# FFN up projection by seven quarter products instead of eight, in a two-layer float32 step

## The chip, the cores and the metric

The kernel runs on one core of one Trainium2 chip. The metric is device time in microseconds (us) from one launch to its end; lower is better. The core has five engines that run side by side, each from its own queue, in order: PE multiplies matrices, DVE and ACT and POOL do elementwise work, SP issues transfers (DMA). [...]

## The reference, cut to what matters

The program is a two-layer decoder step over 1024 prompt tokens and 64 sample tokens, 1088 columns in all. Layer 0 mixes by a recurrence (RWKV), layer 1 by latent attention. Each layer then projects with `w_o`, adds to the residual stream, and runs a gated FFN with a short convolution on the gate:

```python
D_MODEL, D_FF, CONV_W = 1024, 2816, 3

def conv_glu(xn, conv_prev, w_up, conv_w, conv_b, w_down):
    u = xn @ w_up                                  # 1024 x 5632
    gate, val = u[..., :D_FF], u[..., D_FF:]
    ext = concatenate([conv_prev, gate], axis=1)
    conv = conv_b
    for j in range(CONV_W):
        conv = conv + ext[:, j:j + T] * conv_w[j]
    h = silu(conv) * val
    return h @ w_down, ext[:, T:]

# in each layer:
x = x + concatenate([o_tok, o_mem], -1) @ w_o[l]
f, c = conv_glu(rms_norm(x, norm_ffn[l]), ...)
x = x + f
```

## The kernel before, in words

The residual stream lies in SBUF as `x`, 128 partitions x 8 feature blocks x 1088 tokens. All large products are made in float32 precision by splitting each operand in a high and a low part (`wh`, `wl` and `xh`, `xl`, type float32r) and adding three products: `wh*xh + wh*xl + wl*xh`. So a 128 x 128 weight block costs three matmuls for each group of tokens, `gemm_y` at L474 to L476. The split of a weight is a cast on ACT (L207) and a subtraction on DVE (L208; in the first stage, the recurrence, it runs on POOL). The helper `split` (L1130, L1131) does the same for activations. Tokens are taken in three groups `G3` of 364, 364 and 360 columns.

One FFN has 22 chunks of 128 hidden features. For a chunk, `up` loads the gate weights and the value weights (`load_w`, 1024 x 128 each, in two pieces of 256 KB), multiplies the gate (eight blocks of 128 features, three token groups), copies it to `ext` (ACT), runs the convolution over all tokens (DVE, L1300 to L1302), takes SiLU (ACT), multiplies the value part, forms the product and splits it to `hh`, `hl`. Chunks go in six groups of 4, 4, 4, 4, 3, 3. While a group is projected up, the group before it is projected down (`gemm_x`), each result added to `x` by DVE (`residual`, L1159). `merge` interleaves the two streams in program order, by steps and weights:

```python
for i in range(len(groups)):
    u = ups(i)
    if i:
        s.merge([(down(i - 1), 24), (s.take(u, 110), 110)])
    s.drain(u)
return (yield from down_last())
```

The first group has no down projection beside it, and the last down projection (`down_last`) has no up projection beside it. Ahead of the FFN stands the `w_o` projection, whose squares are summed on POOL (`acc`, L1168) for the norm; `norm_x` then scales and splits `x` for the FFN. Behind it stands, in layer 0, the split of `x` for the latent projections, and in layer 1 the final norm. The framework orders the instructions of each engine from the program by its own scheduler; the order tables below show what came out. PSUM has four buffers `mm`, two `dn` and two `tp` in this phase.

Of the kernel before, what the change touches and what calls it, by code (L numbers as in the profile page):

```python
# [85 lines left out]
G3 = [(0, 364), (364, 364), (728, 360)]  # L86
NH = 6
# [10 lines left out]
class Step:  # L98
# [1006 lines left out]
    def load_stream(s, xd, i):  # L1105
        c0, n = G3[i]
        s.tc.keep_in_program_order(s.nc.scalar.dma_start(out=s.x[:, :, c0:c0 + n], in_=xd.rearrange("(k p) t -> p k t", p=128)[:, :, c0:c0 + n]))
# [32 lines left out]
    def load_x(s, first):  # L1140

        nc, x = s.nc, s.x
        for i in range(9):
            rows = 128 if i < 8 else 64
            xt = first[i] if i < len(first) else s.x_tile(i, nc.sync)
            for h in range(2):
                q = s.pst("tp")
                for k in range(4):
                    nc.tensor.transpose(q[:, k * 128:k * 128 + rows], xt[:rows, 512 * h + 128 * k:512 * h + 128 * k + 128], s.ident[:rows, :rows])
                qv = q.rearrange("p (k t) -> p k t", t=128)[:, :, :rows]  # L1150
                nc.scalar.copy(x[:, 4 * h:4 * h + 4, 128 * i:128 * i + rows], qv)
            yield

    def residual(s, d, g, p, acc):
# [7 lines left out]
        a = acc[c0][:, :n]  # L1162
        if d == 0:
            nc.scalar.activation(a, xv, AF.Square)
        else:
            sq = s.st([128, 364], "nt", s.ntb)
# [3 lines left out]
    def last_acc(s):  # L1170

        return s.t(s.wp, [128, 4, 128], "wr", 3).rearrange("p a b -> p (a b)")

    def scales(s, g, acc):
# [4 lines left out]
        nc.tensor.matmul(q[:, :n], s.mean1k, acc[c0][:, :n], start=True, stop=True)  # L1179
        r = s.rstd[c0] = s.t(s.xp, [128, 364], "rstd", 3)[:, :n]  # L1180
# [3 lines left out]
    def norm_x(s, g, acc, gain, xs):  # L1184

        nc = s.nc
        c0, n = g
        for _ in range(s.LAG):
            yield
        s.scales(g, acc)  # L1190
        for k in range(KC):
            xh, xl = xs[k]
            t = s.st([128, 364], "nt", s.ntb)
            nc.vector.scalar_tensor_tensor(t[:, :n], s.x[:, k, c0:c0 + n], s.pv(gain[0], gain[1] + k), s.rstd[c0], ALU.mult, ALU.mult)
            s.split(xh[:, :n], xl[:, :n], t[:, :n])
            yield

    def split_x(s, g, acc, xs):

        c0, n = g  # L1200
        for k in range(KC):
# [3 lines left out]
            if k == s.LAG and g != G3[2]:  # L1205
                s.scales(g, acc)
        if g == G3[2]:
# [3 lines left out]
    def new_xg(s):  # L1211

        xh, xl = (s.t(s.xp, [128, KC, 364], n, 3, F32R) for n in ("xh", "xl"))
        return [(xh[:, k], xl[:, k]) for k in range(KC)]

    def gemm_x(s, wf, xs):

        for d in range(KC):
            w = wf(d)
            for g in G3:  # L1220
                p = s.pst("dn")
                s.drain(s.gemm_y(p, w, xs, *g))
                s.residual(d, g, p, None)
                yield

    def gemm_t(s, ws, d0, xs, acc, after=None, ahead=(), m=8):

        def part(g, x, c0):  # L1230
            for j, w in enumerate(ws):
                p = s.pst("mm")
                s.drain(s.gemm_y(p, w, x, c0, g[1]))
                s.residual(d0 + j, g, p, acc)
# [3 lines left out]
        for i, z in enumerate(xs):  # L1238
            yield from s.mergeg([(part(*z), len(ws)), (pend, m)] + [(a, 8) for a in ahead[i:i + 1]])
            if after:  # L1240
                pend = after(z[0], acc)
        return pend

    def ffn(s, l, xs, pend, after, pre=None):
# [3 lines left out]
        W, Wd = I["w_ffn_up"][l], I["w_ffn_down"][l]  # L1248
        NCH = DFF // 128

# [4 lines left out]
        for i in range(0, NCH, 4):  # L1255
            m = min(4, NCH - i)
            stg = s.st([18, 512], "cvst", 2)
# [3 lines left out]
        nc.scalar.copy(cprev.rearrange("p c b -> p (c b)"), q[:, :16 * NCH])  # L1261

        def up(c, out):
            wg = s.load_w([(W[:, 128 * c:128 * c + 128], 0, 128)])
            if c == 0:
                wv = s.load_w([(W[:, DFF:DFF + 128], 0, 128)])
            yield
            ext = s.st([128, 1106], "ext", 1)
            nc.gpsimd.memset(ext[:, 0:2], 0.0)
            es = ext[:, 1026:1106].rearrange("p (b t) -> p b t", t=10)  # L1270
            nc.gpsimd.tensor_copy(es[:, :, 0:2], cprev[:, c].rearrange("p (b j) -> p b j", j=2))

            def gate(i):
                c0, n = G3[i]
                p = s.pst("mm")
                yield from s.gemm_y(p, wg, xs[i], 0, n)
                m = min(n, NP_ - c0)
                nc.scalar.copy(ext[:, 2 + c0:2 + c0 + m], p[:, :m])  # L1278
                if m < n:
                    nc.scalar.copy(es[:, :, 2:10], p[:, m:n].rearrange("p (b t) -> p b t", t=8))  # L1280

            def val(i):
                p = s.pst("mm")
                yield from s.gemm_y(p, wv, xs[i], 0, G3[i][1])
                ps[i] = p

            ps = {}
            if c == 0:
                for _ in s.seq(gate(0), gate(1), val(0), val(1)):
                    next(pend, None)  # L1290
                    yield
                s.drain(pend)
                yield from gate(2)
            else:
                for i in range(3):
                    yield from gate(i)
            cv = s.st([128, 1106], "cv", 1)
            w = [s.pv(f"conv_w{l}{j}", c) for j in range(3)]
            cv = cv[:, :1104]
            nc.vector.tensor_scalar(cv, ext[:, 0:1104], w[0], s.pv(f"conv_b{l}", c), ALU.mult, ALU.add)  # L1300
            nc.vector.scalar_tensor_tensor(cv, ext[:, 1:1105], w[1], cv, ALU.mult, ALU.add)
            nc.vector.scalar_tensor_tensor(cv, ext[:, 2:1106], w[2], cv, ALU.mult, ALU.add)  # L1302
            nc.scalar.activation(cv, cv, AF.Silu)
            nc.gpsimd.tensor_copy(cout[:, c, 0:2], ext[:, 1024:1026])  # L1304
            nc.gpsimd.tensor_copy(cout[:, c, 2:18].rearrange("p (b j) -> p b j", j=2), es[:, :, 8:10])
            if c:
                wv = s.load_w([(W[:, DFF + 128 * c:DFF + 128 * c + 128], 0, 128)])
            yield
            h, lo = s.st([128, NT], "hh", 6, F32R), s.st([128, NT], "hl", 6, F32R)
            out.append((h, lo))  # L1310
            for i, (c0, n) in enumerate(G3):
                if i not in ps:
                    yield from val(i)
                p = ps.pop(i)
                m = min(n, NP_ - c0)
                t = s.st([128, 364], "nt", s.ntb)
                nc.vector.tensor_tensor(t[:, :m], cv[:, c0:c0 + m], p[:, :m], ALU.mult)
                if m < n:
                    sv = s.bc(cv[:, 1026:1027], [10, 8], [1, 8])
                    nc.vector.tensor_tensor(t[:, m:n].rearrange("p (b t) -> p b t", t=8), sv, p[:, m:n].rearrange("p (b t) -> p b t", t=8), ALU.mult)  # L1320
                s.split(h[:, c0:c0 + n], lo[:, c0:c0 + n], t[:, :n])
                yield

        groups = [(0, 4), (4, 4), (8, 4), (12, 4), (16, 3), (19, 3)]
        hs = {}

        def ups(i):
            c0, n = groups[i]
            hs[i] = []
            for c in range(c0, c0 + n):  # L1330
                yield from up(c, hs[i])

        def down(i):
# [970 lines left out]
```

## Time and profile before

| what | value |
|---|---|
| time, median of 3 runs | 3498.66 us (3494.58 to 3508.95) |
| time of the profiled execution | 3513.38 us |
| its span in the trace | 3511.6 us |
| PE busy in the span | 3368.6 us |
| DVE, ACT, POOL busy | 1790.5, 1298.7, 457.7 us |

The span is what the trace covers from the first to the last instruction. PE's matmuls overlap in the trace (a matmul of 364 columns is shown with some 0.33 us while the next one starts 0.166 us later), so PE's cost is read from the distance between starts, or from a count of matmuls in a stretch in which PE never stops. The layer-0 `w_o` and FFN stage runs from about 985 to 1915 us, that of layer 1 from about 2590 us to the end.

### The profile page before, as it was taken

The page shows a single profiled execution, that of the slowest core. Times are in us where ns is not written, and L with a number is a line of the kernel's source. Part 1 is how long each engine was busy: PE and PEld are TensorE (multiplying, and loading weights), DVE is VectorE, ACT ScalarE, POOL GpSimd, SP SyncE. Part 2 cuts the span into 40 slices and gives each one's busy share as a digit, 9 for nine tenths or more (in the row PEclk, how much of TensorE's full clock was granted, in tenths as well). Part 3 has the DMA queues.
Part 4 walks back from the last instruction along what each step waited for, and adds up shares of the span by engine and source line. Part 5 has one row for each costly group of instructions (what it writes and reads, how often), then busy time and mean ns, then how long its engine had stood idle before and what let it go on. Part 6 is the DMA issues. An engine that isn't in the chain of part 4 may idle for free. (4 is left out here: it accounts for less than half of the span.)

```text
span 3511.6 us, 58202 instructions
## 1 busy us (share of the span) xinstructions
PE 3368.6 (96%) x23112; PEld 2899.4 (83%) x23112; DVE 1790.5 (51%) x4242; ACT 1298.7 (37%) x2971; POOL 457.7 (13%) x767
## 2 busy tenths in 40 slices
PE   6999999999889999999999999899999999999998
PEld 5555677775579999999999888655579999999998
DVE  5776676775535343333345477434445433343344
ACT  5555445543544222212225455333334312222222
POOL 4323133331011000000003001011111000000000
PEclk9998699998889999999999999899999999999999
DMA  4212011113141111111113102345321111111112
GB/s 119 56 39 76 22 39 41 38 47 95 51 153 48 43 49 43 43 46 46 44 46 111 53 28 70 123 163 179 121 75 42 49 49 40 46 46 43 47 44 78
DMA packets 299284, 227.13 MB, mean 65 GB/s; under 512 B 40890, under 2 KB 278222, under 8 KB 294916
## 3 DMA queue, kind: packets, MB, share of 16 engines
q1 hardware_dynamic: 285220, 166.82, 16.3%
q0 software_dynamic: 9888, 51.93, 4.2%
q10 hardware_dynamic: 3904, 4.65, 0.4%
q8 instruction: 182, 2.98, 0.3%
q14 instruction: 90, 0.74, 0.1%
HBM read 197.59 MB, written 25.76 MB: 64 GB/s over the span
## 5 line engine op out<-in xcount | busy, mean ns | idle before, releaser
L474 PE MATMUL pmm<-xh,wh 128*128 128x364 f32 (+2 forms) x2664 | 882.3, 331 | 7.5 <-ACT wh L207 4.8
L476 PE MATMUL pmm<-xh,wl 128*128 128x364 f32 (+2 forms) x2664 | 875.1, 328 | 0.0
L475 PE MATMUL pmm<-xl,wh 128*128 128x364 f32 (+2 forms) x2664 | 872.9, 328 | 0.3
L474 PEld LDWEIGHTS pmm<-xh,wh 128*128 128x128 f32 (+1 forms) x2664 | 500.1, 188 | 12.4 <-ACT wh L207 5.1
L475 PEld LDWEIGHTS pmm<-xl,wh 128*128 128x128 f32 (+1 forms) x2664 | 500.6, 188 | 3.0 <-DVE xl L1434 0.8
L476 PEld LDWEIGHTS pmm<-xh,wl 128*128 128x128 f32 (+1 forms) x2664 | 500.8, 188 | 1.4 <-DVE wl L208 0.2
L207 ACT CAST wh<-wr 128x512 fp32r<-128x512 f32 (+3 forms) x399 | 238.5, 603 | 561.1 <-PE pmm L475 333.4
L208 DVE TENSOR_TENSOR wl<-wr,wh 128x512 fp32r<-128x512 f32 (+2 forms) x307 | 205.0, 670 | 369.9 <-ACT wh L207 369.3
L1159 DVE TENSOR_TENSOR x<-x,pdn 128x364 f32<-128x364 f32 (+1 forms) x240 | 127.4, 531 | 419.2 <-PE pdn L476 419.2
L476 PE MATMUL pdn<-hh,wl 128*128 128x364 f32 (+1 forms) x912 | 300.2, 329 | 0.0
L475 PE MATMUL pdn<-hl,wh 128*128 128x364 f32 (+1 forms) x912 | 298.7, 328 | 0.0
L474 PE MATMUL pdn<-hh,wh 128*128 128x364 f32 (+1 forms) x912 | 298.3, 327 | 0.0
L474 PE MATMUL pmm<-xn,wh 128*128 128x292 f32 (+2 forms) x552 | 207.0, 375 | 3.7 <-DVE e L504 3.7
L475 PE MATMUL pmm<-xn,wh 128*128 128x292 f32 (+2 forms) x552 | 196.9, 357 | 0.0
L476 PE MATMUL pmm<-xn,wl 128*128 128x292 f32 (+2 forms) x552 | 195.5, 355 | 0.6 <-POOL wl L208 0.6
L1278 ACT COPY ext<-pmm 128x364 f32<-128x364 f32 x132 | 58.7, 444 | 364.0 <-PE pmm L476 364.0
L1304 POOL COPY cout<-ext 128x2 f32<-128x2 f32 x44 | 16.9, 385 | 1261.2 <-ACT ext L1278 1261.2
L476 PEld LDWEIGHTS pdn<-hh,wl 128*128 128x128 f32 x912 | 171.3, 188 | 1.1
L475 PEld LDWEIGHTS pdn<-hl,wh 128*128 128x128 f32 x912 | 171.3, 188 | 0.0
L474 PEld LDWEIGHTS pdn<-hh,wh 128*128 128x128 f32 x912 | 171.2, 188 | 0.0
L208 POOL TENSOR_TENSOR wl<-wr,wh 128x512 fp32r<-128x512 f32 (+1 forms) x92 | 121.7, 1325 | 195.9 <-ACT wh L207 163.8
L474 PEld LDWEIGHTS pmm<-xn,wh 128*128 128x128 f32 (+1 forms) x552 | 106.5, 193 | 27.9 <-issue 11.0
(720 smaller groups left out, 5984.1 us busy)
## 6 DMA issues: line engine op xcount, KB each, us to landing
wr<-in_w_ffn_up SPq DMA_DIRECT2D x176, 256.0 KB
wr<-in_w_in_a SPq DMA_DIRECT2D x84, 256.0 KB
wr<-in_w_ffn_down SPq DMA_DIRECT2D x64, 256.0 KB
wr<-in_w_o SPq DMA_DIRECT2D x32, 256.0 KB
wr<-in_w_ffn_down SPq DMA_DIRECT2D x32, 192.0 KB
xl<-odp POOLq DMA_DIRECT2D x4, 1456.0 KB
e<-in_x_prompt SPq DMA_DIRECT2D x16, 256.0 KB
out_y_p<-xl SPq DMA_DIRECT2D x8, 512.0 KB
```

The source lines that it names most:

```text
L207: nc.scalar.copy(wh[:, :n, :m], wr[:, :n, :m])
L208: s.wl_eng.tensor_tensor(wl[:, :n, :m], wr[:, :n, :m], wh[:, :n, :m].bitcast(F32), ALU.subtract)
L474: nc.tensor.matmul(ps[:m, :n], wh[:, :m], xh[:, c0:c0 + n], start=(k == 0), stop=False)
L475: nc.tensor.matmul(ps[:m, :n], wh[:, :m], xl[:, c0:c0 + n], start=False, stop=False)
L476: nc.tensor.matmul(ps[:m, :n], wl[:, :m], xh[:, c0:c0 + n], start=False, stop=(k == last))
L1159: nc.vector.tensor_tensor(xv, xv, p[:, :n], ALU.add)
L1278: nc.scalar.copy(ext[:, 2 + c0:2 + c0 + m], p[:, :m])
L1304: nc.gpsimd.tensor_copy(cout[:, c, 0:2], ext[:, 1024:1026])
```

## The change

The up projection of a chunk is now made for half of the tokens at a time (544), and the half is cut in two quarters of 272 tokens. Gate and value blocks, two halves of the 1024 input features and two token quarters make a 2 x 2 by 2 x 2 block product. It is formed by seven products of combined blocks (Winograd's form of Strassen's scheme) where eight were used. With weights `v1, g1` (first 512 features) and `v2, g2` (last 512) and quarters `lo`, `hi`:

- `load_up` makes four combined weights on POOL (L1281: `s1 = g1 + g2`, `s2 = s1 - v1`, `v1 - g1`, `v2 - s2`) and splits seven weights (ACT L1276, DVE L1277).
- `combine_x` makes the seven combined operands of a half once: DVE scales `x` (L1204), POOL forms four differences (L1207 to L1210), ACT and DVE split all seven. The two halves use the same seven buffers.
- `up` makes seven products of 4 feature blocks x 3 matmuls x 272 columns each (L1333 to L1335) and adds them up on DVE from PSUM and on POOL (L1340). Convolution, SiLU and the product with the value follow on 544 columns (560 in the second half, with the sample tokens).

The 22 chunks are walked twice, once for each half, so all up and down weights are loaded and split twice. The down projection, `w_o` and the latent projections work on quarters of 272 columns as well. In `w_o`, half 0 is projected first, then half 1 while `combine_x` prepares half 0 for the FFN. `combine_x` for half 1 is the beginning of that half's first group of chunks, beside the last down projection of half 0. PSUM is laid out as six `mm` and two `dn`. The core of the diff:

```diff
+    def combine_x(s, h, gain, xs):
+        nc = s.nc
+        xs += [s.new_xq() for _ in range(7)]
+        lo, hi = slice(0, QT), slice(QT, HT)
+        for j in range(4):
+            a = []
+            for k in (j, j + 4):
+                a.append(s.st([128, HT], "tw", 2))
+                nc.vector.scalar_tensor_tensor(a[-1], s.x[:, k, HT * h:HT * h + HT], s.pv(gain[0], gain[1] + k), s.rstd[h], ALU.mult, ALU.mult)
+            yield
+            t = [s.st([128, QT], "nt", s.ntb) for _ in range(4)]
+            nc.gpsimd.tensor_tensor(t[0], a[0][:, hi], a[0][:, lo], ALU.subtract)
+            nc.gpsimd.tensor_tensor(t[1], a[1][:, hi], t[0], ALU.subtract)
+            nc.gpsimd.tensor_tensor(t[2], a[1][:, hi], a[0][:, hi], ALU.subtract)
+            nc.gpsimd.tensor_tensor(t[3], a[1][:, lo], t[1], ALU.subtract)
+            src = (a[0][:, lo], t[1], t[0], t[2], t[3], a[1][:, hi], a[1][:, lo])
+            for (xh, xl), z in zip(xs, src):
+                s.split(xh[:, j], xl[:, j], z)
+                yield
...
+        v1, g1, g2, v2 = piece(fv, 0), piece(fg, 0), piece(fg, 1), piece(fv, 1)
+        yield part(v1)
+        s1 = sub(s.st([128, 4, 128], "ws", 2), g1, g2, ALU.add)
+        s2 = sub(s.st([128, 4, 128], "ws", 2), s1, v1)
+        yield part(s2)
+        yield part(s1)
+        yield part(sub(g1, v1, g1))
+        yield part(g2)
+        yield part(sub(s2, v2, s2))
+        yield part(v2)
...
+            p = yield from product(0)
+            t1 = nt()
+            nc.scalar.copy(t1, p)
+            p = yield from product(1)
+            u2 = nt()
+            add(V, u2, p, t1)
+            p = yield from product(2)
+            t5 = nt()
+            nc.scalar.copy(t5, p)
+            p = yield from product(3)
+            u3 = nt()
+            add(V, u3, p, u2)
...
+                add(P, ext[:, 2 + QT:2 + HT], u3, t5)
+            p = yield from product(4)
+            add(V, ext[:, 2:2 + QT], p, u3)
+            add(P, t5, t5, u2)
...
+            p = yield from product(5)
+            add(V, t[:, QT:], p, t5)
+            p = yield from product(6)
+            add(V, t[:, :QT], p, t1)
...
-                s.merge([(down(i - 1), 24), (s.take(u, 110), 110)])
+        order = [(h, i) for h in range(2) for i in range(len(groups))]
+        for n, z in enumerate(order):
+            u = ups(*z)
+            if n:
+                s.merge([(down(*order[n - 1]), 16), (s.take(u, 64), 64)])
             s.drain(u)
```

DVE around one chunk of layer 0 before, where no down projection runs beside it (`cv` is the convolution, `nt` the product with the value, `wl` a weight's low part):

```order
L208 TENSOR_TENSOR wl_14326<-wr_14323,wh_14325 128x512
L208 TENSOR_TENSOR wl_14346<-wr_14343,wh_14345 128x512
L1300 TENSOR_SCALAR cv_14214<-ext_14132,ptile_195_718 128x1104
L1301 SCALAR_TENSOR_TENSOR cv_14214<-ext_14132,ptile_195_718,cv_14214 128x1104
L1302 SCALAR_TENSOR_TENSOR cv_14214<-ext_14132,ptile_195_718,cv_14214 128x1104
L1317 TENSOR_TENSOR nt_14260<-cv_14214,pmm_14235 128x364
L1131 TENSOR_TENSOR hl_14234<-nt_14260,hh_14233 128x364
L1317 TENSOR_TENSOR nt_14289<-cv_14214,pmm_14264 128x364
L1131 TENSOR_TENSOR hl_14234<-nt_14289,hh_14233 128x364
L208 TENSOR_TENSOR wl_14352<-wr_14349,wh_14351 128x512
```

And DVE now, in a like chunk of one half (`ul` is a weight's low part, `tw` the value part, `wa` and `ws` raw and combined weights):

```order
L1340 TENSOR_TENSOR nt_14925<-pmm_14907,nt_14886 128x272
L1277 TENSOR_TENSOR ul_15031<-ws_15028,uh_15030 128x512
L1340 TENSOR_TENSOR ext_14822<-pmm_14928,nt_14925 128x272
L1277 TENSOR_TENSOR ul_15050<-ws_15026,uh_15049 128x512
L1368 TENSOR_SCALAR cv_14947<-ext_14822,ptile_195_718 128x544
L1340 TENSOR_TENSOR tw_14953<-pmm_14954,nt_14905 128x272
L1369 SCALAR_TENSOR_TENSOR cv_14947<-ext_14822,ptile_195_718,cv_14947 128x544
L1277 TENSOR_TENSOR ul_15070<-wa_15001,uh_15069 128x512
L1370 SCALAR_TENSOR_TENSOR cv_14947<-ext_14822,ptile_195_718,cv_14947 128x544
L1340 TENSOR_TENSOR tw_14953<-pmm_14973,nt_14863 128x272
L1277 TENSOR_TENSOR ul_15090<-wa_15003,uh_15089 128x512
```

A chunk's seven weight subtractions stand between the additions of the products of the chunk ahead of it: the weight of a product is made five products before its turn (there are five buffers `uh`, `ul`).

POOL around a chunk of layer 0 before has only small copies (two chunks are shown, `cout` is the convolution's carry):

```order
L1269 MEMSET ext_14132 128x2
L1271 COPY ext_14132<-cprev_12240 128x8x2
L1304 COPY cout_12241<-ext_14132 128x2
L1305 COPY cout_12241<-ext_14132 128x16
L1269 MEMSET ext_14355 128x2
L1271 COPY ext_14355<-cprev_12240 128x8x2
```

And POOL now, one chunk of half 0:

```order
L1281 TENSOR_TENSOR ws_14590<-wa_14545,wa_14547 128x512
L1281 TENSOR_TENSOR wa_14545<-wa_14543,wa_14545 128x512
L1326 MEMSET ext_14264 128x2
L1281 TENSOR_TENSOR ws_14592<-ws_14590,wa_14543 128x512
L1340 TENSOR_TENSOR ext_14264<-nt_14421,nt_14381 128x272
L1340 TENSOR_TENSOR nt_14381<-nt_14381,nt_14348 128x272
L1376 COPY cout_12655<-ext_14264 128x2
L1281 TENSOR_TENSOR ws_14592<-wa_14549,ws_14592 128x512
```

POOL has taken on six two-input operations in each chunk of each half, and two of them stand between the products and the convolution.

DVE now, in layer 0 at the end of the combination for half 1 (L1134 with `xl`), beside the last down projection of half 0 (`pdn` into `x`):

```order
L1134 TENSOR_TENSOR xl_17549<-nt_17740,xh_17548 128x272
L1162 TENSOR_TENSOR x_11165<-x_11165,pdn_17754 128x272
L1134 TENSOR_TENSOR xl_17555<-tw_17738,xh_17554 128x272
L1134 TENSOR_TENSOR xl_17547<-nt_17741,xh_17546 128x272
L1134 TENSOR_TENSOR xl_17551<-nt_17742,xh_17550 128x272
L1134 TENSOR_TENSOR xl_17553<-nt_17743,xh_17552 128x272
L1134 TENSOR_TENSOR xl_17557<-tw_17738,xh_17556 128x272
L211 TENSOR_TENSOR wl_17779<-wr_17776,wh_17778 128x384
L211 TENSOR_TENSOR wl_17864<-wr_17861,wh_17863 128x384
L211 TENSOR_TENSOR wl_17937<-wr_17934,wh_17936 128x384
L1277 TENSOR_TENSOR ul_18002<-ws_17843,uh_18001 128x512
```

Eight of the 16 down results of that projection are added ahead of the last row of the combination (the one shown is the eighth); the weights of the other eight (`wl`) are split behind it.

## Rows read from the trace of the kernel before

**Rows 1.** The page, its span and engines: busy us, share, instructions.
```profile
span 3511.6 us, 58202 instructions
...
PE 3368.6 (96%) x23112; PEld 2899.4 (83%) x23112; DVE 1790.5 (51%) x4242; ACT 1298.7 (37%) x2971; POOL 457.7 (13%) x767
```
**Rows 2.** Busy time by stretch: both FFNs and a stretch of decode.
```profile
core 0: us, PE busy (x) PEld busy (x) DVE busy (x) ACT busy (x) POOL busy (x), PEclk, DMA share, GB/s
1130.00:1860.00 730.00, 730.00 (x4407) 729.44 (x4406) 290.80 (x465) 164.19 (x302) 17.97 (x86) 1.00 0.16 45
2735.00:3450.00 715.00, 715.00 (x4316) 714.44 (x4315) 280.69 (x449) 156.62 (x289) 16.89 (x82) 1.00 0.16 45
2200.00:2400.00 200.00, 188.78 (x1182) 114.18 (x1183) 87.67 (x242) 72.53 (x208) 24.88 (x26) 0.96 0.43 147
```
**Rows 3.** PE's waits from 975 to 2000 us and from 2590 us on.
```profile
PE ptp L1149 <- DMA xt<-in_x_prompt: 8.0, 2, 7.4
...
PE pmm L474 <- ACT wh L207: 4.8, 1, 4.8
```
**Rows 4.** PE's groups by form: line, tiles, shape, count; busy us, mean ns.
```profile
L474 PE MATMUL pmm<-xh,wh 128*128 128x364 f32 x1760 | 585.5, 333 | 7.5 <-ACT wh L207 4.8 <-ACT xh L1433 2.6
L474 PE MATMUL pmm<-xh,wh 128*128 128x360 f32 x880 | 288.1, 327 | 0.0
L476 PE MATMUL pdn<-hh,wl 128*128 128x364 f32 x608 | 201.1, 331 | 0.0
L476 PE MATMUL pdn<-hh,wl 128*128 128x360 f32 x304 | 99.2, 326 | 0.0
```
**Rows 5.** PE in order of time: start us, duration us, 256 columns (layer 1's end).
```profile
3489.76 0.28 PE L475 MATMUL pmm<-hl,hh 128*128 128x256 f32 x1
...
3490.96 0.28 PE L476 MATMUL pmm<-hh,hl 128*128 128x256 f32 x1
```
**Rows 6.** The same for 292 columns, first and last of 55 (first stage).
```profile
408.75 0.30 PE L474 MATMUL pmm<-xn,wh 128*128 128x292 f32 x1
...
416.00 0.30 PE L474 MATMUL pmm<-xn,wh 128*128 128x292 f32 x1
```
**Rows 7.** DVE's groups by form, 1130 to 1860 us.
```profile
L208 DVE TENSOR_TENSOR wl<-wr,wh 128x512 fp32r<-128x512 f32 x115 | 79.5, 691 | 138.0 <-ACT wh L207 137.9
L1159 DVE TENSOR_TENSOR x<-x,pdn 128x364 f32<-128x364 f32 x80 | 42.6, 532 | 128.8 <-PE pdn L476 128.8
L1301 DVE SCALAR_TENSOR_TENSOR cv<-ext,ptile,cv 128x1104 f32<-128x1104 f32 x22 | 30.1, 1368 | 0.7
L1300 DVE TENSOR_SCALAR cv<-ext,ptile 128x1104 f32<-128x1104 f32 x22 | 18.7, 851 | 0.0
```
**Rows 8.** DVE in order of time: two weight subtractions back to back, merged.
```profile
1004.56 1.29 DVE L208 TENSOR_TENSOR wl<-wr,wh 128x512 fp32r<-128x512 f32 x2 [10.62 <-ACT wh L207]
```
**Rows 9.** ACT's groups by form, 1130 to 1860 us.
```profile
L207 ACT CAST wh<-wr 128x512 fp32r<-128x512 f32 x115 | 71.0, 620 | 209.2 <-PE pmm L475 129.0 <-PE pdn L475 76.3 <-ACT ext L1280 3.9
L1303 ACT ACTIVATE cv<-cv 128x1104 f32<-128x1104 f32 x22 | 24.8, 1127 | 78.3 <-DVE cv L1302 78.3
```
**Rows 10.** POOL's groups by form, whole span.
```profile
L208 POOL TENSOR_TENSOR wl<-wr,wh 128x512 fp32r<-128x512 f32 x88 | 119.4, 1360 | 186.4 <-ACT wh L207 162.6 <-PE pmm L476 10.0 <-ACT q L911 2.4
...
L1168 POOL TENSOR_TENSOR acc<-acc,nt 128x364 f32<-128x364 f32 x28 | 29.2, 1044 | 128.7 <-ACT nt L1167 128.7
```
**Rows 11.** DVE in order of time, end of layer 0's FFN.
```profile
1878.58 1.09 DVE L1131 TENSOR_TENSOR xl<-x,xh 128x364 fp32r<-128x364 f32 x1 [0.58 <-ACT xh L1130]
1879.60 0.52 DVE L1159 TENSOR_TENSOR x<-x,pmm 128x364 f32<-128x364 f32 x1
1880.04 0.87 DVE L1131 TENSOR_TENSOR xl<-x,xh 128x364 fp32r<-128x364 f32 x1
...
1881.28 0.52 DVE L1131 TENSOR_TENSOR xl<-x,xh 128x364 fp32r<-128x364 f32 x1
```
**Rows 12.** POOL in the same stretch: two additions, merged.
```profile
1878.31 2.21 POOL L1168 TENSOR_TENSOR cv<-cv,nt 128x364 f32<-128x364 f32 x2 [1.58 <-ACT nt L1167]
```

More of the change, by code (lines that the diff above doesn't have):

```diff
@@ L86 @@
 G3 = [(0, 364), (364, 364), (728, 360)]
+HT = NT // 2
+QT = NT // 4
+G4 = [(QT * i, QT) for i in range(4)]
 NH = 6
@@ L1218, in gemm_x, with new_xg @@
+    def new_xg(s, last=False):
+        q = s.new_xq(), tuple(s.st([128, 4, QT], z, 1, F32R) for z in ("xh", "xl")) if last else s.new_xq()
+        return [(xh[:, k], xl[:, k]) for xh, xl in q for k in range(4)]
+    def gemm_x(s, wf, xs, h, acc=None, tag="dn"):
         for d in range(KC):
             w = wf(d)
[L1220 to L1223, printed above, removed]
+            for i in range(2):
+                p = s.pst(tag)
+                s.drain(s.gemm_y(p, w, xs[i], 0, QT))
+                s.residual(d, G4[2 * h + i], p, acc)
@@ L1261, in ffn @@
         nc.scalar.copy(cprev.rearrange("p c b -> p (c b)"), q[:, :16 * NCH])
[L1263 to L1266, printed above, removed]
-            yield
[L1268 to L1322, printed above, removed]
@@ L1324, in ffn, with ups @@
         groups = [(0, 4), (4, 4), (8, 4), (12, 4), (16, 3), (19, 3)]
         hs = {}
-        def ups(i):
+        operands = [xs0, []]
+        def ups(h, i):
             c0, n = groups[i]
-            hs[i] = []
+            hs[h, i] = []
+            if h and i == 0:
+                yield from s.combine_x(1, ("norm_ffn", 8 * l), operands[1])
             for c in range(c0, c0 + n):
-                yield from up(c, hs[i])
-        def down(i):
+                yield from up(h, c, operands[h], hs[h, i])
@@ new lines, in quarters, with down @@
+        def quarters(x):
+            return [[(a[:, QT * i:QT * i + QT], b[:, QT * i:QT * i + QT]) for a, b in x] for i in range(2)]
+        def down(h, i):
+            acc = None
+            if l == 0 and i == len(groups) - 1:
+                acc = s.new_acc(h)
+            yield from s.gemm_x(lambda d: wd(i, d), quarters(hs.pop((h, i))), h, acc)
+            if i == len(groups) - 1:
+                if l == 0:
+                    for g in G4[:2]:
+                        s.scales(g, acc)
@@ L1351, in down_last @@
             if pre:
                 pre()
[L1353 to L1365 removed]
+            acc = s.new_acc(1) if l == 0 else None
@@ L1366, in ffn @@
+            first = s.seq(*[after(g, None) for g in G4[:2]])
+            return (yield from s.gemm_t(ws, hs.pop((1, i)), acc, after, [[first, s.conv_out(l, cout)], []]))
+        order = [(h, i) for h in range(2) for i in range(len(groups))]
[3 more added lines that the diff above has]
+                s.merge([(down(*order[n - 1]), 16), (s.take(u, 64), 64)])
             s.drain(u)
@@ L1445, in trunk_tail @@
[L1445 to L1450 removed]
+                s.merge([(project(0), 17), (parts(os_[1]), 16)])
+                s.merge([(project(1), 17), (s.combine_x(0, ("norm_ffn", 8 * l), xs), 32)])
@@ L1572, in latents @@
         for w in ck:
-            for i in range(2):
+            for i in range(3):
                 s.drain(gemm(w, i))
@@ L1584, in along @@
             for w in ws:
-                for i in range(3):
+                for i in range(4):
                     for _ in gemm(w, i):
```

277 lines of the change are left out of this document (165 added, 112 removed).

## The prediction

> **What bounds the kernel now.** I read the page first, then busy time by stretch. DVE is busy for half of the span [rows 1], but an average over stages says little here, so the FFN is read by itself: from 1130 to 1860 us PE is busy for 730.00 of 730 us at full granted clock, and the same holds in layer 1, while DVE is at 40%, ACT at 22% and POOL at 2% [rows 2]. PE's waits in the `w_o` and FFN stages are few: the largest two are for a transfer at layer 0's start and for a weight cast at layer 1's start, and none stands inside an FFN [rows 3]. So the FFN lasts as long as PE's matmuls do, and whatever the change does to the other engines costs nothing until they become later than PE.
>
> The price of a matmul is read from starts, since durations overlap: 4407 in 730 us is 0.1656 us each, at a mean of 362.7 columns [rows 2].
>
> **What it removes.** The counts of one of `gemm_y`'s three lines are 2640 into `mm` and 912 into `dn` [rows 4]. Times three that is 7920, of which the code gives 6336 to the up projection, 1152 to `w_o` and 432 to the latents, and 2736; with 432 of the two last down projections and 72 of a narrow latent block, 11160 matmuls. After the change: up 2 x 22 x 2 x 7 x 4 x 3 = 7392, down 4224, `w_o` 1536, latents 672, together 13824, all of 272 columns.
>
> No row shows 272 columns. At 256 columns ten matmuls start in 1.20 us, 0.120 each [rows 5]; at 292, 54 intervals take 7.25 us, 0.1343 each [rows 6]. Between them 272 comes to 0.1264, and on the line from 256 to the FFN's 362.7 to 0.1268. I take 0.1265. [...] So 11160 x 0.1656 = 1848 us becomes 13824 x 0.1265 = 1749 us: **99 us less** (81 to 131). The up projection alone loses 114 us; the finer quarters in down, `w_o` and latents give 15 back.
>
> **What it adds.** Prices first. A weight subtraction of 512 columns occupies DVE for 0.60 us (two end 1.29 us after the first starts, one lasts 0.69) [rows 7, 8]; 364 columns take 0.44 from start to start [rows 11]. On that line 272 take 0.34 and 544 take 0.64. The convolution's passes at half length are some 0.45 + 2 x 0.69 [rows 7]. POOL takes 1.36 us for 512 columns and 1.04 for 364, so some 0.84 for 272 [rows 10].
>
> For one chunk of one half (PE: 84 x 0.1265 = 10.6 us of up projection):
> - DVE operations with both inputs in SBUF: seven weights 4.2, convolution 1.8, product and split 1.3; 7.3 us. Additions from PSUM: 5 x 0.34 = 1.7.
> - POOL: 4 x 1.36 + 2 x 0.84 = 7.1 us, where it had only small copies.
> - ACT: seven casts of 0.62, half a SiLU and copies [rows 9], some 6.5 us, covered.
> - Transfers: four pieces of 256 KB, with two for the down projection 1.57 MB in 16.7 us, 94 GB/s. The trace carries 147 GB/s over 200 us of decode [rows 2], so I cost the doubled loading at nothing.
>
> DVE alone (9.0 us) would stay under PE. But DVE and POOL don't run side by side. A split of `x` that takes DVE 0.52 us alone takes 1.09 and 0.87 when a POOL addition is running, and the latter ends at 1880.91, 0.39 us after POOL's two additions end (1878.31 + 2.21): it did its 364 columns after POOL had let go. The addition from PSUM at 1879.60 keeps its 0.52 us with POOL running [rows 11, 12]. So I add up POOL's time and DVE's two-SBUF time, and let the PSUM additions run beside POOL where the order allows. [...] By this the chunk needs 14.4 us (16.1 with no PSUM addition hidden); POOL's row means hold some of its own waiting for DVE, so I take 13.8. It follows, per layer:
>
> - **First group of half 0.** No down projection stands beside it: 4 x (13.8 - 10.6) = 13 us of PE waiting for weights. Below: 3 (only the two chained POOL combinations ahead of the second product); above: 4 x 5.5 = 22.
> - **The other groups**, ten times four chunks. PE has 4 x (10.6 + 6.1) = 66.8 us with the down projection. DVE's two-SBUF work is 4 x 7.3 + 8 x 0.60 = 34.0, POOL's 25.6 to 28.4, the PSUM additions 12.2. The pair needs 59.6 to 74.6, in the middle 67.1, next to PE. By the merge weights (16 steps beside 64, 29 steps a chunk) the down projection runs beside the first 2.2 chunks only; the other 1.8 fall behind by 1.8 x 3.2 = 5.8 us, which the five weights made ahead just cover (four products of 1.5 us). I take 0.7 us a group, 7 us a layer. Bounds: nothing, and 7.8 a group.
> - **Change of halves.** `combine_x` for half 1 writes the buffers that half 0's last chunk reads, so it starts when that chunk's products end. It has DVE at 8 x 0.69 + 28 x 0.34 = 15 us and POOL at 16 x 0.84 = 13, with the last chunk's rest (2.5) and eight down results (2.7) in DVE's queue. Some 25 us pass until the first product's operands are complete, allowing for what runs beside. PE has four of eight down blocks meanwhile, 72 x 0.1265 = 9 us; the other four wait for weights queued behind the combination on DVE. 16 us of waiting. Below 7 (DVE alone), above 25 (all in a row, with layer 0's squares on POOL too).
> - **Start, `w_o` and end.** `combine_x` for half 0 has 49 us of `w_o` as cover, less some 8 us for the norm's chain: 4 us. Bounds 0 and 10. This cover gone, it would cost as much as the change of halves.
>
> Sum: 40 us a layer, 80 us. -99 + 80 = -19. The profiled execution took 3513.38 us (span 3511.6), 15 us over the median; I apply the difference to the median: 3498.66 - 19 = **3480 us**.
>
> **Rivals.**
> 1. *The exclusion is cheap.* POOL's work falls into DVE's idle moments, since DVE waits for products anyway. For it: in the FFN as it was DVE idles 60% [rows 2]. Against: DVE goes to 70% or more by itself. Stalls of 3 + 0 + 7 + 0 a layer: -99 + 20 = -79, 3420 us.
> 2. *DVE and POOL become the bound of the FFN* (slower). Place: the groups with a down projection. If only a quarter of the PSUM additions run beside POOL, the pair needs some 70 us for four chunks against 66.8, 3 us a group and 30 a layer; the first group then loses 18, the change of halves 22, the rest 8. 2 x 78 = 156, so +57: 3556 us. It decides from about 68.5 us per four chunks on, where the 99 us are used up. For it: rows 11 and 12 show the exclusion as total, and DVE's queue is in order, so that PSUM additions behind a blocked subtraction wait too. Against: the five products of lead.
> 3. *Narrower matmuls don't start sooner*, because each loads its own weights. Weight loads are busy for 729.44 of 730 us in the FFN [rows 2]. If these set the pace, 13824 x 0.1656 = 2289 us, 441 more: 3940 us. Against: matmuls of 256 columns, each with its own load, start every 0.120 us [rows 5]. [...]
>
> **How the numbers follow.** The forecast's case gets 0.45 (its own range 3450 to 3510), rival 1 0.25 (3395 to 3450), rival 2 0.26 (3510 to 3590), rival 3 0.04. Half a per cent, 17.5 us, is about what a measurement of this kernel can tell from no change. Faster by more (below 3481): rival 1 and a little over half of the forecast's case, 0.49. Within: 0.25. Slower: most of rival 2, and rival 3, 0.26. The range that leaves out 2 in 10 reaches into both neighbours, 3415 to 3560; their far ends and the matmul price's bounds lie beyond.
>
> **What would show it.** Starts of matmuls of 272 columns 0.125 to 0.128 us apart where PE isn't waiting. PE no longer at 100% in the FFN: waits for `ul` (DVE) and for combined weights in the first four chunks of half 0, some 13 us, and a hole of 10 to 20 us at the change of halves, in each layer. DVE's weight subtractions lengthened from 0.69 to above 1 us on the mean where POOL runs, and PSUM additions not. If the subtractions keep 0.69 us, rival 1 holds; if PE waits evenly in all groups, rival 2. The prediction is wrong if the groups in the middle lose much more or less than 1 us each, or if a stage that I left at nothing (transfers, ACT, PSUM buffers) shows up among PE's waits.

## The result, and the profile after

The changed kernel takes **3700.68 us** (median of 4, 3689.83 to 3708.91), where the kernel before, timed beside it, takes 3500.57: 1.057 times as long (interval 1.053 to 1.060). I had forecast 3480 us with a range up to 3560 and gave "slower" 26 in 100. The prediction was wrong in sign and size.

The page of the changed kernel, its span and engines:

```profile
span 3698.9 us, 68167 instructions
...
PE 3347.9 (91%) x25782; PEld 2856.5 (77%) x25782; DVE 2666.0 (72%) x5485; ACT 1634.0 (44%) x3664; POOL 1256.6 (34%) x1524
```

Against [rows 1] PE is busy for 20.7 us less in a span that is 187 us longer. It waits now, and its waits have these names (engine, line, tile, what ended the wait; us in all, times, longest):

```profile
PE pdn L477 <- ACT hh L1133: 110.6, 22, 6.8
PE pmm L1335 <- DVE ul L1277: 30.5, 39, 2.4
PE pmm L1152 <- DMA xt<-in_x_prompt: 20.3, 5, 7.7
PE pdn L1189 <- POOL acc L1171: 15.0, 7, 3.7
...
PE pmm L1333 <- ACT xh L1133: 11.4, 10, 2.7
```

Of these, [rows 3] has only the transfer, with 8.0 us. The largest is a place of which the prediction does not speak: the first down matmul that reads `hh` of a group's last chunk. It comes at all ten changes of groups of each layer, with 3.1 to 6.8 us. Layer 0 by stretches (columns as in [rows 2]): the first group of four chunks, the first chunk after a change of groups, the next chunk, the last two of that group, the first chunk after the next change, and the change of halves:

```profile
1128.40:1185.60 57.20, 49.92 (x345) 47.92 (x346) 52.54 (x64) 25.29 (x47) 37.22 (x33) 0.89 0.32 92
1185.60:1215.30 29.70, 23.81 (x173) 23.27 (x172) 24.09 (x33) 8.34 (x15) 13.87 (x14) 0.89 0.22 63
1215.30:1236.40 21.10, 21.10 (x170) 21.10 (x169) 16.22 (x26) 7.31 (x15) 8.08 (x8) 1.00 0.32 95
1236.40:1260.60 24.20, 24.12 (x191) 23.90 (x190) 23.83 (x36) 12.66 (x24) 11.30 (x12) 1.00 0.36 101
1260.60:1290.30 29.70, 23.82 (x173) 23.28 (x172) 23.76 (x33) 8.31 (x15) 13.87 (x14) 0.89 0.23 66
...
1519.20:1628.10 108.90, 89.05 (x588) 82.32 (x587) 100.22 (x150) 57.53 (x118) 69.11 (x76) 0.91 0.31 90
```

The price of a matmul is read from the third row: 168 start between the first matmul of that chunk (1215.33 us) and of the next (1236.46), 0.1258 us each, and 0.1263 is the mean over the stretches without a wait. What a stretch holds beyond its count times 0.126 is lost: 57.2 - 345 x 0.126 = 14 us in the first group, 29.7 - 173 x 0.126 = 8 us in the fifth row, 35 us at the change of halves, nothing in the third and fourth. So a group runs at PE's pace inside and loses 8 us where it begins: 6 us of waiting, and some 2 us by which the matmuls behind the wait are slower, at a lower granted clock (0.89 in that row on the mean; 0.50 from 1344.70 to 1348.00 us, behind the wait shown next, where a matmul starts every 0.23 us instead of 0.126).

One such change, in order of time (start us, duration us), first PE, around its wait:

```profile
1334.76 0.29 PE L1335 MATMUL pmm<-xh,ul 128*128 128x272 f32 x1
1334.88 0.29 PE L477 MATMUL pdn<-hh,wh 128*128 128x272 f32 x1
...
1338.67 0.28 PE L1333 MATMUL pmm<-xh,uh 128*128 128x272 f32 x1
1344.70 0.82 PE L477 MATMUL pdn<-hh,wh 128*128 128x272 f32 x2 [5.75 <-ACT hh L1133]
1345.32 0.43 PE L1334 MATMUL pmm<-xl,uh 128*128 128x272 f32 x1
1345.55 0.43 PE L1335 MATMUL pmm<-xh,ul 128*128 128x272 f32 x1
```

ACT, from SiLU to the cast:

```profile
1342.42 0.66 ACT L1371 ACTIVATE cv<-cv 128x544 f32<-128x544 f32 x1 [6.84 <-DVE cv L1370]
...
1344.00 0.65 ACT L1133 CAST hh<-tw 128x544 fp32r<-128x544 f32 x1 [0.42 <-DVE tw L1389]
```

DVE, the convolution's three passes and what stands between them:

```profile
1336.13 1.01 DVE L1368 TENSOR_SCALAR cv<-ext,ptile 128x544 f32<-128x544 f32 x1
1337.07 0.43 DVE L1340 TENSOR_TENSOR tw<-pmm,nt 128x272 f32<-128x272 f32 x1
1337.42 1.60 DVE L1369 SCALAR_TENSOR_TENSOR cv<-ext,ptile,cv 128x544 f32<-128x544 f32 x1
1338.94 1.75 DVE L1277 TENSOR_TENSOR ul<-wa,uh 128x512 fp32r<-128x512 f32 x1
1340.61 1.78 DVE L1370 SCALAR_TENSOR_TENSOR cv<-ext,ptile,cv 128x544 f32<-128x544 f32 x1
```

POOL in the same stretch, an addition of the chunk and three combinations of the next:

```profile
1335.74 1.10 POOL L1340 TENSOR_TENSOR nt<-nt,nt 128x272 f32<-128x272 f32 x1
...
1337.15 1.29 POOL L1281 TENSOR_TENSOR ws<-wa,ws 128x512 f32<-128x512 f32 x1
1338.39 1.74 POOL L1281 TENSOR_TENSOR ws<-wa,wa 128x512 f32<-128x512 f32 x1
1340.22 1.59 POOL L1281 TENSOR_TENSOR wa<-wa,wa 128x512 f32<-128x512 f32 x1
```

Read it from POOL's rows. The three combinations run from 1337.15 to 1341.81. The convolution's second pass starts at 1337.42, and ends at 1339.02, 0.58 us after the first combination (1338.44). The weight subtraction behind it ends at 1340.69, 0.56 us after the second (1340.13), and the third pass at 1342.39, 0.58 us after the third (1341.81). Alone such a DVE operation takes 0.60 us ([rows 8], a weight subtraction) to 0.69 (a pass of the convolution in the run with all on DVE, below) from start to start. So each did its work when a POOL operation had ended, and POOL then let one DVE operation past. Only then can SiLU, the product and the cast to `hh` follow, which ends at 1344.65. PE had started the last matmul of the chunk's seventh product at 1334.76; it ran 31 matmuls of other work, the first of them the down matmuls of the three earlier chunks, started the last of these at 1338.67, and starts again at 1344.70, at first 0.23 us a matmul. The addition from PSUM (`pmm`, into which PE writes) at 1337.07 keeps 0.43 us.

### The profile page after: what moved, and what is told of

The parts are those of the page before. It is cut to its first block, busy times and chain, and to the rows that moved or that the text cites. A ratio compares the mean times of both kernels' runs of the same rounds, so it can differ in the third digit from the quotient of the medians.

```text
span 3698.9 us, 68167 instructions
## 1 busy us (share of the span) xinstructions
PE 3347.9 (91%) x25782; PEld 2856.5 (77%) x25782; DVE 2666.0 (72%) x5485; ACT 1634.0 (44%) x3664; POOL 1256.6 (34%) x1524
## 5 line engine op out<-in xcount | busy, mean ns | idle before, releaser
L1335 PE MATMUL pmm<-xh,ul 128*128 128x272 f32 x2464 | 733.0, 298 | 30.7 <-DVE ul L1277 30.5
L1333 PE MATMUL pmm<-xh,uh 128*128 128x272 f32 x2464 | 725.4, 295 | 18.8 <-ACT xh L1133 11.4
L1334 PE MATMUL pmm<-xl,uh 128*128 128x272 f32 x2464 | 727.6, 295 | 4.9 <-DVE xl L1134 4.6
L1335 PEld LDWEIGHTS pmm<-xh,ul 128*128 128x128 f32 x2464 | 479.1, 194 | 40.7 <-DVE ul L1277 40.4
L1333 PEld LDWEIGHTS pmm<-xh,uh 128*128 128x128 f32 x2464 | 477.6, 194 | 22.3 <-ACT xh L1133 14.0
L477 PE MATMUL pdn<-hh,wh 128*128 128x272 f32 x1312 | 388.2, 299 | 113.8 <-ACT hh L1133 110.6
L1334 PEld LDWEIGHTS pmm<-xl,uh 128*128 128x128 f32 x2464 | 480.6, 195 | 7.8 <-DVE xl L1134 7.6
L478 PE MATMUL pdn<-hl,wh 128*128 128x272 f32 x1312 | 393.5, 300 | 6.2 <-DVE hl L1134 4.0
L479 PE MATMUL pdn<-hh,wl 128*128 128x272 f32 x1312 | 390.6, 298 | 0.0
L1277 DVE TENSOR_TENSOR ul<-wa,uh 128x512 fp32r<-128x512 f32 x352 | 309.4, 888 | 60.4 <-ACT uh L1276 59.0
L1276 ACT CAST uh<-wa 128x512 fp32r<-128x512 f32 x352 | 213.7, 618 | 200.1 <-PE pmm L1334 164.8
L1340 POOL TENSOR_TENSOR ext<-nt,nt 128x272 f32<-128x272 f32 (+2 forms) x132 | 119.1, 916 | 437.8 <-ACT uh L1276 252.4
L1277 DVE TENSOR_TENSOR ul<-ws,uh 128x512 fp32r<-128x512 f32 x264 | 225.1, 853 | 20.0 <-ACT uh L1276 11.0
L1276 ACT CAST uh<-ws 128x512 fp32r<-128x512 f32 x264 | 160.8, 618 | 170.0 <-PE pmm L1334 130.9
L1281 POOL TENSOR_TENSOR ws<-ws,wa 128x512 f32<-128x512 f32 x88 | 115.7, 1315 | 315.8 <-DVE ul L1277 315.6
```

The costliest lines, as they stand in the source:

```text
L477: nc.tensor.matmul(ps[:m, :n], wh[:, :m], xh[:, c0:c0 + n], start=(k == 0), stop=False)
L478: nc.tensor.matmul(ps[:m, :n], wh[:, :m], xl[:, c0:c0 + n], start=False, stop=False)
L479: nc.tensor.matmul(ps[:m, :n], wl[:, :m], xh[:, c0:c0 + n], start=False, stop=(k == last))
L1276: nc.scalar.copy(wh, w)
L1277: eng.tensor_tensor(wl, w, wh.bitcast(F32), ALU.subtract)
L1333: nc.tensor.matmul(p, wh, xh[:, k], start=k == 0, stop=False)
```

## The experiments

Theory after the result: the last chunk's tail, from its last product to its `hh`, is late, by POOL's combinations. Rival: DVE and POOL together simply have too much to do. The kernel before, timed beside each run, took 3493 to 3502 us, so a difference of two runs' times holds to some 10 us; the ratios are to that kernel.

**Later down projection.** If only the place of the wait counts, work put ahead of it hides it.

```
             if n:
+                if z != (1, 0):
+                    s.drain(s.take(u, 16))
                 s.merge([(down(*order[n - 1]), 16), (s.take(u, 64), 64)])
```

> Sixteen steps (48 matmuls, 6.1 us) of the next group's up projection are emitted ahead of the down projection, at every change of groups but the change of halves. Theory (late tail: at a change of groups PE stands at the first down matmul that reads the last chunk's hh, 6.0 us, and then runs some 13 to 17 matmuls at the lower clock, 8 to 9 us in all, nine such changes a layer): those losses go, 9 x 7 to 8.5 us a layer, 2 layers, -125 to -150 us, 3550 to 3575 us. Rival (DVE and POOL together are the bound of the groups): the wait only moves to ul and ext, gain under 40 us, above 3660 us.

Measured 3613.46 us, 1.034 (1.031 to 1.038): 87 us of the 125 to 150 expected. From 1182 to 1460 us PE still waits for `hh` and `hl`:

```profile
PE pdn L478 <- DVE hl L1134: 6.0, 4, 1.5
PE pdn L477 <- ACT hh L1133: 5.3, 4, 1.3
```

The place is right, but neither figure of the expectation, which also counts nine changes a layer where there are ten. Six microseconds of cover do not quite hide the tail, and it got no shorter: at the second to fourth change of layer 0 it lasts 9.5 to 9.7 us from the start of the last matmul of the last product to the end of the cast to `hh`, against 9.9 in the changed kernel. The wait for `hl`, the low part, which comes after it, shows as well.

**Combinations on DVE.** The same amount of results, on the engine that was already the fuller one.

```
-            nc.gpsimd.tensor_tensor(o, a, b, op)
+            nc.vector.tensor_tensor(o, a, b, op)
```

> The four weight combinations of a chunk run on DVE (some 0.60 us each) instead of POOL (1.29 us each, during which DVE's two-input operations stand). Theory with the exclusion: the pair's work falls by 4 x (1.29 - 0.60) = 2.8 us a chunk, the convolution's passes fall from 1.0, 1.6 and 1.8 us to some 0.55, 0.79 and 0.79, the wait for hh at a change of groups shrinks from 6.0 to some 3 to 4 us and the first group's losses (13.6 us) halve: -50 to -90 us, 3610 to 3650 us. Rival (DVE's own queue is the bound, since it goes from 72% busy to more): slower than the changed kernel, 3705 to 3760 us.

Measured 3511.76 us, 1.005 (1.003 to 1.007). That is 189 us less than the changed kernel, more than twice what I expected, and nearly all of the 200 by which that kernel is slower. The rival fell: the tail at those changes lasts 4.9 us, and DVE's busy time even went down, from 2666.0 to 2596.2 us, with 352 instructions more. With the up projection's additions moved as well:

```
-            V, P = nc.vector, nc.gpsimd
+            V = P = nc.vector
```

> As the run with the combinations on DVE, and the additions of the up projection that ran on POOL (0.77 us alone, 1.09 beside DVE) are on DVE too (some 0.35 us each). Theory with the exclusion: a further 0 to 30 us less than with the combinations alone, 3590 to 3645 us. Rival (DVE's queue is the bound): 10 to 40 us more than with the combinations alone.

Measured 3501.68 us, 1.002 (1.000 to 1.004): 10 us less than the run before, inside the expected step of 0 to 30, though the time misses its range as that run's did. The changes of groups cost nothing any more (1.5 and 2.9 us in all in the two layers). The tail is down to 3.2 us, less than the 3.9 us of other work that PE had in the change shown above. The chunk after a change takes 21.5 us for 172 matmuls (columns as above):

```profile
1259.60:1281.10 21.50, 21.50 (x172) 21.50 (x172) 21.13 (x41) 9.50 (x17) 0.68 (x2) 1.00 0.37 106
```

and the convolution's last two passes ahead of it, in DVE's order of time, run unhindered:

```profile
1257.38 0.78 DVE L1369 SCALAR_TENSOR_TENSOR cv<-ext,ptile,cv 128x544 f32<-128x544 f32 x1
1258.07 0.43 DVE L1340 TENSOR_TENSOR tw<-pmm,nt 128x272 f32<-128x272 f32 x1
1258.42 0.78 DVE L1370 SCALAR_TENSOR_TENSOR cv<-ext,ptile,cv 128x544 f32<-128x544 f32 x1
```

**Both.** The first edit and the last together.

> Both: the down projection 16 steps later, and all combinations and additions of the up projection on DVE. Theory: the gain of the later down projection (125 to 150 us) and what of the other remains outside the changes of groups (first groups, change of halves: 15 to 40 us): 3515 to 3555 us. Rival (what the later down projection brought is lost again to a fuller DVE): at or above the run with the later down projection alone.

Measured 3494.36 us, 1.000 (0.998 to 1.003), below the range. The later down projection, worth 87 us while POOL combined, is worth 7 here, within the intervals of the two.

**Is it POOL's running, or that the combinations come late from POOL?** Moving them changes both. So POOL was given the work back with nobody waiting for its results.

```
             nc.vector.tensor_tensor(o, a, b, op)
+            nc.gpsimd.tensor_tensor(dm, dm, dm, op)
```

> The combinations run on DVE, as in the second run (3512 us), and POOL does the same four operations of 512 columns a chunk once more on a scratch tile of zeros that nobody else reads or writes. Theory (POOL's operations hold up DVE's two-input operations while they run, whatever they compute): the convolution's passes and the weight subtractions lengthen again to some 1.6 to 1.8 us, the wait for hh at the changes of groups comes back, and most of the 189 us is lost again: 3640 to 3760 us. Rival (what cost was the combinations' own delay on POOL, 1.29 us each in a chain ahead of the casts): nobody waits for the scratch tile, so 3505 to 3540 us.

Measured 3805.91 us, 1.089 (1.085 to 1.093), above the theory's range. The direction is the theory's, but the run doesn't prove it: the scratch operations depend on nothing and ran ahead (all 176 of layer 0's lie between 1130 and 1900 us, with 35 of the 44 additions into `nt`), and between 1144 and 1400 us DVE's convolution waited for an addition on POOL:

```profile
DVE cv L1372 <- POOL ext L1344: 71.3, 6, 26.2
```

So the same again without POOL's own results in the chain (base: all on DVE, 3501.68 us), the scratch operations paced by the weights' transfers:

```
         yield part(v1)
+        for z in (v1, g2, v2, g2):
+            nc.gpsimd.tensor_tensor(dm, z, z, ALU.subtract)
```

> A cleaner form of the run with scratch operations, since there the scratch tile depended on nothing and filled POOL's queue ahead of the additions that the convolution waits for. Here all combinations and additions are on DVE (3502 us), and POOL subtracts four raw weight pieces a chunk into a scratch tile that nobody reads, each piece when its transfer has landed, so that they keep the pace of the chunks. Theory (POOL's two-input operations shut out DVE's): the wait for hh at each change of groups and the waits of the first groups come back, 3600 to 3720 us. Rival (the cost in the run before came from POOL's queue alone): 3495 to 3530 us.

Measured 3647.38 us, 1.040 (1.037 to 1.044): 146 us more than the base (134 by the ratios), for results that nobody reads. No instruction waits for the scratch operations, and of the transfers' waits from 1206 to 1500 us only one of 1.0 us is for POOL, and that for a copy, so they don't hold up the weights' buffers either. From 1206 to 1500 us PE's wait of the changed kernel is back, where the base has 0.3 us of waits in the same groups:

```profile
PE pdn L477 <- ACT hh L1133: 12.1, 4, 3.7
```

DVE in order of time in this run, two operations from SBUF and one from PSUM:

```profile
1289.20 1.52 DVE L1277 TENSOR_TENSOR ul<-wa,uh 128x512 fp32r<-128x512 f32 x1
1290.65 1.52 DVE L1281 TENSOR_TENSOR ws<-ws,wa 128x512 f32<-128x512 f32 x1
1292.10 0.42 DVE L1162 TENSOR_TENSOR x<-x,pdn 128x272 f32<-128x272 f32 x1
```

POOL's scratch operations beside them, three merged:

```profile
1288.67 4.41 POOL L1289 TENSOR_TENSOR dm<-wa 128x512 f32<-128x512 f32 x3 [3.64 <-DMA wa<-in_w_ffn_up]
```

The two from SBUF take 1.52 us each, the one from PSUM 0.42, and the tail at those changes is 6.9 to 7.1 us again. What costs is that POOL runs, not when its results come.

**The change of halves.** Two sizes of it, on the kernel of 3494.36 us. First without the combination of half 1, which then multiplies by the operands of half 0:

```
-                yield from s.combine_x(1, ("norm_ffn", 8 * l), operands[1])
+                operands[1] = xs0
```

> The run with a later down projection and all on DVE (3494 us), with the operands of the second token half left out: that half multiplies by the first half's operands. Theory: the change of halves costs 25 to 30 us a layer in waits for these operands, 3430 to 3445 us. By the 16 us a layer of my prediction 3460 us. Rival (the wait would be for the down projection's weights and sums anyway): above 3475 us.

Measured 3445.51 us, 0.986 (0.983 to 0.989): 49 us, 24 to 25 a layer on the mean: just under the theory's 25 to 30, and above my 16. That is nearly all of what the two changes of halves lost in the run that it builds on: summed by chunk, as told under (a) below, 31 us in layer 0 and 19 in layer 1. Second, the additions of the combination on DVE, and layer 0's transposes on the other PSUM tag:

```
-            nc.gpsimd.tensor_tensor(t[0], a[0][:, hi], a[0][:, lo], ALU.subtract)
+            nc.vector.tensor_tensor(t[0], a[0][:, hi], a[0][:, lo], ALU.subtract)
...
-                q = s.pst("mm")
+                q = s.pst("dn")
```

> The run with a later down projection and all on DVE (3494 us), with two edits more: the 16 operand additions of each token half run on DVE instead of POOL, and the transposes of x ahead of layer 0's w_o take PSUM buffers of the other tag, so that w_o's matmuls needn't follow behind all of them. Theory: of some 30 us lost at each change of halves 5 to 10 us go, and of the 20 to 35 us that layer 0's w_o starts later than before 10 to 25 us: 3450 to 3480 us. Rival (DVE's queue is what lasts at the change of halves, and the transposes wait for their transfer anyway): 3488 to 3505 us.

Measured **3470.88 us, 0.993 (0.991 to 0.996)**: faster than the kernel before, too. At layer 0's change of halves 31 us were lost with all on DVE (106.2 us with 597 matmuls, the first row below), and 23 are in this run (106.0 with 655, the second). Summed by chunk it goes from 31 to 26, and in layer 1 from 19 to 15. The transposes have the larger part. Counted from the last matmul into `pso`, in the stage ahead of `w_o` (what comes before it varies by over 20 us between executions), layer 0's first product starts 163 us later here, 163 and 165 in the two runs below, which have the same edit, and 178 to 181 in the changed kernel and every run without it; the kernel before has 145. So the other PSUM tag is worth some 15 us of the 24.

```profile
1485.70:1591.90 106.20, 88.89 (x597) 81.84 (x596) 100.39 (x181) 55.81 (x114) 37.28 (x48) 0.94 0.30 89
```

The same stretch of this run:

```profile
1484.00:1590.00 106.00, 94.88 (x655) 88.67 (x655) 100.79 (x207) 59.49 (x121) 18.84 (x34) 0.95 0.32 96
```

In both DVE is busy for 95% of that stretch: it is what lasts there. Placing the down projection more densely beside it should then do nothing:

```
-                s.merge([(down(*order[n - 1]), 16), (s.take(u, 64), 64)])
+                s.merge([(down(*order[n - 1]), 16), (s.take(u, 64), 64 if z != (1, 0) else 36)])
```

> The version with the operand additions on DVE and the transposes in the other PSUM tag (3471 us), with the down projection at the change of halves emitted more densely: 16 of its steps beside 36 steps of the next group instead of 64, so that 14 instead of 8 stand beside the combination. If PE there waits because the down projection's work is placed too late, 5 to 15 us less: 3455 to 3466 us. If DVE, which has the combination and the down projection's weights and sums, is what lasts, no difference: 3466 to 3478 us.

Measured 3484.63 us, 0.994 (0.992 to 0.997), against 0.993: no difference that can be told, as the second case has it, though the time itself lies above its range. The intervals alone would leave room for a gain of some 8 us, but the changes of halves lose 28 and 18 us here, and 26 and 15 without the edit. Last of these, the version of 3470.88 us without the later down projection:

```
             if n:
-                if z != (1, 0):
-                    s.drain(s.take(u, 16))
```

> The same version as 3471 us without the later down projection. Theory (with the combinations off POOL the last chunk's hh is ready in time, the loss at a change of groups is 1 us or less): 3470 to 3480 us. Rival (the lead of 16 steps is needed still): above 3490 us.

Measured 3478.83 us, 0.993 (0.990 to 0.995). The lead isn't needed once POOL's work is on DVE: from 1185 to 1470 us the view of the waits lists none of PE's.

**The seven products alone undone.** Eight plain products in the same two halves; the core of the edit:

```
-        yield part(v1)
-        s1 = sub(s.st([128, 4, 128], "ws", 2), g1, g2, ALU.add)
...
+        ps = [piece(fg, 0), piece(fg, 1), piece(fv, 0), piece(fv, 1)]
+        for z in ps:
+            yield part(z)
...
-            src = (a[0][:, lo], t[1], t[0], t[2], t[3], a[1][:, hi], a[1][:, lo])
+            src = (a[0][:, lo], a[0][:, hi], a[1][:, lo], a[1][:, hi])
```

> Only the seven products are undone: eight plain products in the same two token halves, four weight pieces a chunk instead of seven, no combinations of weights or tokens. Theory: 1056 matmuls more at 0.1265 us are 134 us more than the run with everything on DVE and no waits inside groups, from which the waits of the first groups and some of the change of halves fall away (15 to 30 us a layer): 3570 to 3600 us, less than the changed kernel's 3701 us although PE has more to do. Rival (the two passes themselves cost what was lost, by loading all weights twice and by the change of halves): above 3660 us.

Measured 3562.00 us, 1.020 (1.016 to 1.023), 8 us below the range. Layer 0's FFN shows PE at full clock and busy for all but 2.4 of 780 us:

```profile
1130.00:1910.00 780.00, 777.63 (x6151) 774.65 (x6151) 422.31 (x755) 264.74 (x512) 46.55 (x145) 1.00 0.30 88
```

So inside the FFN the two passes, the doubled weight loading and the change of halves as such cost next to nothing. What was lost there hangs on the combinations, and mostly on the engine that made them. The late starts don't: without any combination layer 0's first product still comes 178 us after the last matmul into `pso`, where the kernel before has 145. That, 7 us at layer 1's start and 31 us for narrower matmuls (14880 x 0.1263 us against 1848) are most of what this run is slower by.

## Why the prediction was wrong, point by point

- **The matmuls: right.** 13824 x 0.1263 = 1746 us against 1848, so 102 us less, where I had 99. No run shows the two prices behind the bounds of 81 and 131; what the runs showed is 0.1258 to 0.1263 us a matmul. Rival 3 is out: matmuls of 272 columns start every 0.126 us while the weight loads are busy for all of the stretch (21.10 of 21.10 us). They were as full with starts 0.1656 us apart [rows 2], so their busy share doesn't tell here that weight loads set PE's pace.
- **The prices: right**, as far as they go. Subtractions of 512, 272 and 544 columns start 0.60, 0.35 and 0.64 us apart when POOL is still (I had 0.60, 0.34, 0.64), a POOL combination that doesn't wait takes 1.29 us, an addition 0.77 to 1.1 (1.36, 0.84).
- **That DVE and POOL exclude each other: right**, and shown now by scratch work alone. A combination on DVE takes 0.69 us in the run with all on DVE and 1.52 beside POOL's scratch operations; in the rows of the change of groups the DVE operations from SBUF take 1.60 to 1.78 us and each ends 0.56 to 0.58 us after one of POOL's.
- **(a) First group: the sum is right, in part by luck.** 13 us forecast, 13.6 and 13.5 measured. (These losses are summed by chunk: the time from its first matmul to the next chunk's first, less 0.1263 us for each matmul between.) But the working has 3.2 us in each chunk, and layer 0 lost 7.3, 0.0, 3.6 and 2.7. And only some 4 us of it hang on POOL: with all on DVE 9.4 and 9.7 us are still lost, about 5 in the first chunk and 1.5 in each other, where DVE's own sum, 9.0 + 4 x 0.60 + 2 x 0.35 = 12.1 us, exceeds PE's 10.6.
- **(b) The ten other groups: this step failed.** I forecast 7 us a layer with bounds of 0 and 78; 87 and 88 were lost. The working compared sums: four chunks of the pair's work against four chunks of PE's, with five weights of lead to even out. The sums were fair (inside the groups nothing is lost, and in the last two chunks DVE is busy for 23.83 of 24.20 us). But a sum says nothing on latency. The down projection needs the *last* chunk's `hh` 31 matmuls, 3.9 us, after that chunk's last product, and three POOL combinations for the next chunk, 1.29, 1.74 and 1.59 us in the rows above, stand in the middle of the convolution that makes it. I priced the convolution as 1.8 us of work and never followed its end to the instruction that waits for it. Rival 2 had the right engine pair, but as throughput in all chunks, so 3556 us; PE does not wait evenly, but once a group. What the runs show in place of the 7 us is the tail: 9.9 us in the changed kernel, 4.9 and 3.2 with POOL's work moved to DVE, 7.1 with scratch work on POOL.
- **(c) Change of halves: right place, too small.** 16 us with bounds of 7 and 25, against 35 and 29. With the weight combinations and the up projection's additions on DVE 31 and 19 are lost, with the operand additions there too 26 and 15. So part of the excess is the same exclusion; without it layer 0 still loses more than I forecast, and layer 1 does not.
- **(d) Start and end: too small.** 4 us a layer with a bound of 10, against 33 in layer 0 and 11 in layer 1. In each layer some 9 us pass in PE's gaps between `w_o` and the first product. Layer 0 has more: the kernel before puts the transposes of `x` into `tp` buffers of their own, between `w_o`'s first matmuls, and the changed one into `mm`, so that `w_o` starts behind all of them (36 us later, counted from the last matmul into `pso`). PE's wait for the transfers of `x` goes from 8.0 us [rows 3] to 20.3. The prediction left PSUM buffers at nothing; giving the transposes the other tag won some 15 us back.

In sum, against the profiled execution before: -102 for the matmuls; losses of 14 + 87 + 35 in layer 0 and 14 + 88 + 29 in layer 1; 33 and 11 at the starts. That is +209. The stages ahead of layer 0's `w_o`, which the change leaves alone, took 12 us less in this execution (the last matmul into `pso` starts at 948.5 us, before at 960.6): +197, where the spans differ by 187. The other 10 us were not traced.

## What to carry to other kernels

When work is added on two engines that hold each other up, as DVE and POOL do here (1.52 us beside POOL for an operation of 0.69 alone), put it on one of them, even on the fuller one: here four additions a chunk cost DVE 2.4 us, and cost 189 us of time as POOL's operations of 1.29 us, each of which held up a DVE operation for its length in the rows above. A budget of busy time per stage must be followed by a second question: which result does the bounding engine need first at each boundary, and what stands between its last input and it. Trading an eighth of the matmuls for additions can pay, but little: with every combination on DVE the gain of some 100 us shrinks to 0.7%, since the late starts, the first groups and the changes of halves take the rest, and DVE is then the limit at the changes of halves. And look at what a new layout of buffers does outside the changed loop: the transposes' PSUM tag cost 15 us far from any combination.

## What the runs showed that I had not expected

- One-input operations from SBUF to SBUF are held too, not only those with two inputs: the convolution's first pass takes 1.01 us beside POOL's addition (its row above ends 0.30 us after the addition does), and 0.56 us on the mean in the run with all on DVE.
- The two engines take turns one instruction each in the change of groups shown (POOL's 1.29, 1.74 and 1.59 us, DVE's 1.60, 1.75 and 1.78). Small POOL instructions seem to suffer as well, though no run tested it alone. With all on DVE, POOL's groups by form have a copy of 16 columns at 1.57 us on the mean, ahead of the convolution, and one of the same size at 0.37 behind it:

```profile
L1324 POOL COPY ext<-cprev 128x16 f32<-128x16 f32 x22 | 34.4, 1565 | 0.0
...
L1374 POOL COPY cout<-ext 128x16 f32<-128x16 f32 x22 | 8.1, 370 | 0.7 <-DVE ext L1340 0.7
```

- In the changed kernel a wait of 6 us cost PE some 8: the matmuls after it started 0.23 us apart, at a granted clock of 0.50, and the chunk's mean is 0.89.
